# Lp pooling, p = 2: the last, smallest store is queued on SP behind two held stores instead of on ScalarE

## The chip, the cores and the metric

The kernel runs on one core of one Trainium2 chip. The metric is the device time of one execution in microseconds (us). Within one batch of runs the kernel before varied from 395.26 to 395.89 us, so differences below about 0.5 us (0.13%) can't be read from single times; for those the traces are compared piece by piece.

## The reference

For an array `x` of 32 x 256 x 4096 float32, each window of four neighbours gives the square root of the mean of its squares. 134.22 MB are read and 33.55 MB written.

```python
for i in range(out_length):                      # out_length = 1024, kernel_size = 4, p = 2
    window = np.abs(x[:, :, 4*i : 4*i+4]) ** p
    result[:, :, i] = (np.mean(window, axis=-1)) ** (1.0 / p)
```

## The kernel before

The input is seen as 32 blocks of 128 partitions x 8192 elements (4 MB each). SP (SyncE) loads the blocks, ScalarE squares half a block at a time, VectorE adds groups of four, and ScalarE takes the square root, one half block behind. Blocks are grouped for the stores: seven groups of four blocks (4 MB of output each), one of three (3 MB), and the last block alone (1 MB, 8 KB per partition). The stores of groups 0 to 5 are issued on ScalarE. The stores of groups 6 and 7 are *held*: SP issues them after all its loads. The last store (group 8) is on ScalarE.

```python
    groups += [(j, 1) for j in range(n - LAST, n)]
    held = {len(groups) - 1 - LAST - j for j in range(2)}       # groups 6 and 7
    # ... (pools and helpers cut) ...
    def root(i, c):
        # ... o is this half block's part of the group's output tile ot ...
        nc.scalar.activation(
            out=o, in_=o, func=mybir.ActivationFunctionType.Sqrt, scale=1.0 / k,
        )
        if i == first + g - 1 and c + CH == W and group_of[i] not in held:
            nc.scalar.dma_start(out=out_block(group_of[i]), in_=ot)
    # ... main loop: load(i + 3), square, reduce, root of the half block before ...
    root(*pending)
    for gi in sorted(held):
        nc.sync.dma_start(out=out_block(gi), in_=ots[gi])
```

Of the kernel before, what the change touches and what calls it, by code (L numbers as in the profile page):

```python
# [1 line left out]

# [4 lines left out]


@with_exitstack
def kernel(  # L10
    ctx: ExitStack,
    tc: tile.TileContext,
    x: bass.AP,
    p: float,
    kernel_size: int,
    out: bass.AP,
):








    nc = tc.nc

    assert float(p) == 2.0, "kernel specialized for p == 2"
    k = int(kernel_size)
    assert k == 4, "kernel specialized for kernel_size == 4"  # L30

    P = nc.NUM_PARTITIONS
    fp32 = mybir.dt.float32
    xf = x.rearrange("b c l -> (b c l)")
    of = out.rearrange("b c l -> (b c l)")
    total = xf.shape[0] // P

    W = 8192
    CH = 4096
    GROUP = 4  # L40
    LAST = 1
    n = total // W
    assert n * W == total


    groups = []
    i = 0
    while i < n - LAST:
        g = min(GROUP, n - LAST - i)
        groups.append((i, g))  # L50
        i += g
    groups += [(j, 1) for j in range(n - LAST, n)]
    held = {len(groups) - 1 - LAST - j for j in range(2)}
    group_of = {}
    for gi, (first, g) in enumerate(groups):
        for j in range(g):
            group_of[first + j] = gi

    in_pool = ctx.enter_context(tc.tile_pool(name="in_pool", bufs=4))
    out_pool = ctx.enter_context(tc.tile_pool(name="out_pool", bufs=2))  # L60
    last_pool = ctx.enter_context(tc.tile_pool(name="last_pool", bufs=1))
    ctx.enter_context(tc.manual_schedule())


    def x_block(i):
        first, g = groups[group_of[i]]
        block = xf[first * W * P:(first + g) * W * P].rearrange("(p w) -> p w", p=P)
        return block[:, (i - first) * W:(i - first + 1) * W]

    def out_block(gi):  # L70
        first, g = groups[gi]
        return of[first * W * P // k:(first + g) * W * P // k].rearrange("(p w) -> p w", p=P)

    xts = {}
    ots = {}

    def load(i):
        xt = in_pool.tile([P, W], fp32)
        nc.sync.dma_start(out=xt, in_=x_block(i))  # L79
        xts[i] = xt  # L80

    def root(i, c):
        first, g = groups[group_of[i]]
        ot = ots[group_of[i]]
        at = ((i - first) * W + c) // k
        o = ot[:, at:at + CH // k]
        nc.scalar.activation(  # L87
            out=o, in_=o, func=mybir.ActivationFunctionType.Sqrt, scale=1.0 / k,
        )
        if i == first + g - 1 and c + CH == W and group_of[i] not in held:  # L90
            nc.scalar.dma_start(out=out_block(group_of[i]), in_=ot)

    for i in range(3):
        load(i)

    pending = None
    for i in range(n):
        if i + 3 < n:
            load(i + 3)
        gi = group_of[i]  # L100
        first, g = groups[gi]
        if i == first:
            pool = last_pool if i >= n - LAST else out_pool
            ot = pool.tile([P, g * W // k], fp32)
            ots[gi] = ot
        for c in range(0, W, CH):
            xh = xts[i][:, c:c + CH]
            nc.scalar.activation(  # L108
                out=xh, in_=xh, func=mybir.ActivationFunctionType.Square,
            )  # L110
            at = ((i - first) * W + c) // k
            nc.vector.tensor_reduce(  # L112
                out=ots[gi][:, at:at + CH // k],
                in_=xh.rearrange("p (n j) -> p n j", j=k),
                axis=mybir.AxisListType.X, op=mybir.AluOpType.add,
            )
            if pending is not None:
                root(*pending)
            pending = (i, c)
    root(*pending)  # L120
    for gi in sorted(held):
        nc.sync.dma_start(out=out_block(gi), in_=ots[gi])


# [1 line left out]
_INS = ['x', 'p', 'kernel_size']  # L126
_OUTS = [((32, 256, 1024), 'float32')]

_NUMBERS = {'p': 2.0, 'kernel_size': 4}


# [26 lines left out]
```

## Time and profile before

| | before |
|---|---|
| median time | 395.74 us (395.67 to 395.85, 3 runs) |
| span of the profiled execution | 393.7 us |
| share of 16 DMA engines' span taken by both data queues | 83.9% + 15.5% = 99.4% |
| ScalarE (ACT), VectorE (DVE) busy | 75%, 72% |
| last square root ends | 387.23 us |
| last store: issued, landing | 387.26 us, 5.6 us after its issue |

From the page of the kernel before: engine totals, the DMA row (tenths of the mean busy share, 40 slices of the span), and the DMA queues (q1 belongs to SP, q10 to ScalarE; packets, MB, share of 16 engines' span).

```profile
span 393.7 us, 357 instructions
DVE 282.8 (72%) x64; ACT 294.7 (75%) x130; POOL 0.2 (0%) x4
...
DMA  8999998999999999999999999999999999999997
...
q1 hardware_dynamic: 4896, 141.56, 83.9%
q10 hardware_dynamic: 1008, 26.21, 15.5%
...
out_dram<-ot SPq DMA_DIRECT2D x1, 3072.0 KB, 12.3
out_dram<-ot ACTq DMA_DIRECT2D x1, 1024.0 KB, 5.6
```

The DMA engines are the limit: they are busy for 90% or more in all but the first, the seventh and the last slice. The last two lines give size and time from issue to landing (the moment at which the completion of the transfer shows in the trace) of the 3 MB store and of the last store. Only the end of the span can react to this change, so here is the timeline of that end (start, duration, engine, line, what; in brackets the idle time before it and who ended it).

```profile
377.27 8.87 DVE L112 TENSOR_REDUCE ot<-xt 128x1024 f32<-128x4096 f32 x2 [0.84 <-ACT xt L108]
378.09 3.60 ACT L108 ACTIVATE xt<-xt 128x4096 f32<-128x4096 f32 x1
381.72 1.06 ACT L87 ACTIVATE ot<-ot 128x1024 f32<-128x1024 f32 x1
386.17 1.06 ACT L87 ACTIVATE ot<-ot 128x1024 f32<-128x1024 f32 x1 [3.40 <-DVE ot L112]
387.26 0.34 ACTq L91 DMA_DIRECT2D out_dram<-ot  x1
```

Last comes what SP waits for (total us, times, longest us): line 122 is the held stores, line 153 the end of the program.

```profile
SPq L122 <- ACT ot L87: 30.2, 2, 28.7
SPq L153 <- DMA out_dram<-ot: 14.1, 2, 9.6
```

The trace also records each DMA packet (start, duration, queue, size), which is where the end can be watched in detail. It doesn't name the DMA engine, so an engine's sequence has to be matched by ends and starts (they lie within 8 ns of each other). "Runs out" below means the end of an engine's last 24 KB packet of the 3 MB store; the time given is that of the engine's completion record there.

### The profile page before, as it was taken

What the parts mean: (1) busy time and instruction counts of PE and PEld (TensorE: products, weight loads), DVE (VectorE), ACT (ScalarE), POOL (GpSimd) and SP (SyncE); (2) the same over time, 40 slices, a digit from 0 to 9 for tenths busy, and PEclk for the clock granted to TensorE, in tenths of its full rate; (3) what the DMA queues carried; (4) which work ended last, traced back from release to release, by engine and by line L of the source; (5) the groups of instructions that cost most, each with busy time, mean ns of one, the idle gap of its engine ahead of it and who ended that gap; (6) DMA issues with size and microseconds to landing.
All of it is one profiled execution on the core that took longest, in us unless ns stands there. A gap on an engine that the chain in (4) does not pass through costs nothing.

```text
span 393.7 us, 357 instructions
## 1 busy us (share of the span) xinstructions
DVE 282.8 (72%) x64; ACT 294.7 (75%) x130; POOL 0.2 (0%) x4
## 2 busy tenths in 40 slices
DVE  0399996739976399764988559866598846999992
ACT  1699987469883798828988189863998819999981
POOL 0000000000000000000000000000000000000000
DMA  8999998999999999999999999999999999999997
GB/s 350 446 430 426 426 426 373 449 446 430 433 426 426 426 430 453 440 430 433 426 426 426 426 449 443 427 433 430 426 426 426 443 446 433 430 433 426 426 435 314
DMA packets 5906, 167.79 MB, mean 426 GB/s; under 512 B 656, under 2 KB 656, under 8 KB 656
## 3 DMA queue, kind: packets, MB, share of 16 engines
q1 hardware_dynamic: 4896, 141.56, 83.9%
q10 hardware_dynamic: 1008, 26.21, 15.5%
q14 instruction: 2, 0.02, 0.0%
HBM read 134.22 MB, written 33.55 MB: 426 GB/s over the span
## 4 chain that ended last, share of the span: by engine, by line
DMA 72%; ACT 17%; DVE 9%; SPq 0%; issue 0%; ACTq 0%
DMA xt<-in_x_dram 72%; ACT xt L108 14%; DVE ot L112 9%; ACT ot L87 2%; SPq L79 0%; ACTq L108 0%
## 5 line engine op out<-in xcount | busy, mean ns | idle before, releaser
L112 DVE TENSOR_REDUCE ot<-xt 128x1024 f32<-128x4096 f32 x64 | 282.8, 4420 | 103.4 <-ACT xt L108 102.6
L108 ACT ACTIVATE xt<-xt 128x4096 f32<-128x4096 f32 x64 | 230.9, 3610 | 87.6 <-DMA xt<-in_x_dram 85.0
L87 ACT ACTIVATE ot<-ot 128x1024 f32<-128x1024 f32 x64 | 67.0, 1047 | 4.2 <-DVE ot L112 3.4
L108 ACT ACT_TABLE_LOAD x1 | 1.3, 1283 | 0.7 <-PEq L139 0.7
L87 ACT ACT_TABLE_LOAD x1 | 1.3, 1283 | 0.0
L139 POOL MEMSET const-uint8-127<- 128x1 uint8 x1 | 0.1, 102 | 0.0
L139 POOL MEMSET const-bfloat16-1.0<- 128x1 bf16 x1 | 0.1, 101 | 0.0
L139 POOL MEMSET const-float32-0.0<- 128x1 f32 x1 | 0.1, 98 | 0.2 <-issue 0.2
L139 POOL MEMSET const-float32-1.0<- 128x1 f32 x1 | 0.1, 98 | 0.0
## 6 DMA issues: line engine op xcount, KB each, us to landing
xt<-in_x_dram SPq DMA_DIRECT2D x32, 4096.0 KB, 35.9
out_dram<-ot ACTq DMA_DIRECT2D x6, 4096.0 KB, 23.2
out_dram<-ot SPq DMA_DIRECT2D x1, 4096.0 KB, 34.1
out_dram<-ot SPq DMA_DIRECT2D x1, 3072.0 KB, 12.3
out_dram<-ot ACTq DMA_DIRECT2D x1, 1024.0 KB, 5.6
```

What stands on the lines that cost most here:

```text
L87: nc.scalar.activation(out=o, in_=o, func=mybir.ActivationFunctionType.Sqrt, scale=1.0 / k,)
L108: nc.scalar.activation(out=xh, in_=xh, func=mybir.ActivationFunctionType.Square,)
L112: nc.vector.tensor_reduce(out=ots[gi][:, at:at + CH // k], in_=xh.rearrange("p (n j) -> p n j", j=k), axis=mybir.AxisListType.X, op=mybir. ...
L139: nc = _bacc.Bacc("TRN2", target_bir_lowering=False, num_devices=1)
```

## The change

The intent is to take the last DMA issue off ScalarE and to let all three late stores follow one another in SP's queue.

```diff
     held = {len(groups) - 1 - LAST - j for j in range(2)}
+    late = held | set(range(len(groups) - LAST, len(groups)))
@@ root()
-        if i == first + g - 1 and c + CH == W and group_of[i] not in held:
+        if i == first + g - 1 and c + CH == W and group_of[i] not in late:
             nc.scalar.dma_start(out=out_block(group_of[i]), in_=ot)
@@ the end
     root(*pending)
-    for gi in sorted(held):
+    for gi in sorted(late):
         nc.sync.dma_start(out=out_block(gi), in_=ots[gi])
```

## The prediction

> **What bounds the kernel now.** The 16 DMA engines. The page's slices show DMA at 0.9 or more almost throughout; its queue table adds up to 99.4% of 16 engines' span (83.9% + 15.5%), 426 GB/s over 393.7 us for 167.79 MB. ACT (75%) and DVE (72%) have slack; the chain of waits is 72% input loads. Only the end could change. The timeline there: last reduction 381.72 to 386.14, last square root 386.17 to 387.23, last store issued on ScalarE 387.26 to 387.60, landing 5.6 us after its issue, closing waits, end 393.7.
>
> **What is removed, added, moved.** One DMA issue leaves ScalarE (0.34 us, the last thing it does), one joins SP (0.34 us, as SP's other two stores take). The instruction order of both builds shows nothing else moved: each transfer keeps its semaphore, and the moved store still waits only for the last root. SP is free by then (its 3 MB store was issued at 378.2 to 378.6) and need not wait for the stores ahead to land. So the issue moves from 387.26 to about 387.3: one cross-engine semaphore step.
>
> **The bytes.** They are the same on the same 16 engines. The Trainium skill, "DMA: Bandwidth & Descriptors", section "Issuing engines are not separate DMA queues", says that transfers run on the same 16 engines whoever issues them, and that only sequencer issue time is saved. The packet records agree: the 3 MB store (24 KB packets, 912 ns) keeps all engines full until 388.94; then 15 run out one by one (the last at about 389.5) and one lags to 390.10. (Records do not name the engine; I match ends with starts.) Each goes straight on to 8 KB packets, with no gap to remove. The lagging engine ends last: its eight packets of 309 ns (2.47 us) begin at 390.11 and end at 392.56, so the handover between queues costs nothing on the engine that decides. The other 15 lose 0.1 to 0.4 us in slowed packets (up to 746 ns) between 389.55 and 390.2, and are still done by 392.0. If one queue removes that, it is off the critical path.
>
> Queueing behind the held stores costs nothing either: the 4 MB one is gone by 382.8, and the 3 MB one is drained first today too.
>
> **On the critical path:** about 0; the semaphore step (estimate +0.05 us) is hidden as long as descriptors arrive before the lagging engine runs out at 390.1 (now the first packet starts at 388.9, 1.3 us after the issue ended).
>
> **Predicted time:** 395.7 us; 8 in 10 between 395.2 and 396.3. Faster by over 2%: 0.5%; within 2%: 99%; slower by over 2%: 0.5%.
>
> **Signs.** Right: the ScalarE issue row of 1,024 KB goes, an SP row of 1,024 KB comes, issued near 387.3, landing in 5.2 to 5.9 us; all 8 KB packets on the first queue, after the 24 KB ones; the last ends near 392.5; the timeline to 387.2 is unchanged. Wrong: SP issues only after another store has landed (after 390); a gap ahead of the 8 KB packets on the lagging engine, or the slowed packets reaching it (up to +0.4 us); a landing under 5 us, meaning that one queue drains faster than two.
>
> **What would make it wrong.** The lag of that engine (0.6 us) may depend on what the queues did; if it vanishes, some 0.5 us is gained and the slowed packets become critical. A hidden limit on transfers queued by SP could delay the last issue. Both are far below 2%.

Its packet times are all 0.08 us late, because a wrong zero point was taken for them (388.94, 390.10, 390.11 and 392.56 should read 388.86, 390.02, 390.03 and 392.48); durations and order are not touched. The timeline's own times are right.

## The result, and the profile after

| | before | after |
|---|---|---|
| median time | 395.71 us (395.51 to 395.85, 6 runs) | 395.59 us (395.32 to 395.83, 6 runs) |
| ratio, 95% interval | | 0.9997 (0.9985 to 1.001): same |
| span of the profiled execution | 393.68 us | 393.30 us |
| last square root starts | 386.17 us | 385.79 us |
| from there to the end of the span | 7.50 us | 7.51 us |

From the page of the changed kernel (the same lines):

```profile
span 393.3 us, 357 instructions
DVE 282.8 (72%) x64; ACT 294.7 (75%) x130; POOL 0.2 (0%) x4
...
DMA  9999999999999999999999999999999999999997
...
q1 hardware_dynamic: 5040, 142.61, 84.5%
q10 hardware_dynamic: 864, 25.17, 14.8%
...
out_dram<-ot SPq DMA_DIRECT2D x1, 3072.0 KB, 12.3
out_dram<-ot SPq DMA_DIRECT2D x1, 1024.0 KB, 5.6
```

1.05 MB moved from q10 to q1, and the landing of the last store is 5.6 us after its issue, as before. The end of the timeline, after:

```profile
376.88 8.87 DVE L113 TENSOR_REDUCE ot<-xt 128x1024 f32<-128x4096 f32 x2 [0.84 <-ACT xt L109]
377.70 3.60 ACT L109 ACTIVATE xt<-xt 128x4096 f32<-128x4096 f32 x1
381.33 1.06 ACT L88 ACTIVATE ot<-ot 128x1024 f32<-128x1024 f32 x1
385.79 1.06 ACT L88 ACTIVATE ot<-ot 128x1024 f32<-128x1024 f32 x1 [3.39 <-DVE ot L113]
386.87 0.33 SPq L123 DMA_DIRECT2D out_dram<-ot  x1
```

Every line is 0.38 to 0.39 us earlier than before, the last issue included. So the whole 0.38 us by which the profiled spans differ lies before the last root, in a part that the change does not touch; behind it the two agree within 0.01 us. SP's waits, after:

```profile
SPq L123 <- ACT ot L88: 38.9, 3, 28.7
SPq L154 <- DMA out_dram<-ot: 5.1, 1, 5.1
```

SP waits for the root in line 123 for 8.7 us more (38.9 against 30.2), and at the end of the program for 9.0 us less (5.1 against 14.1). It is the same idle time, taken in another line: before, SP stood in its closing wait while ScalarE issued the last store.

The packet records of the last microseconds (times in us from the span's start):

| | before | after |
|---|---|---|
| last store's data could start (issue + 0.85 us, measured in the first experiment) | 388.11 | 387.72 |
| first DMA engine runs out of 24 KB packets | 388.85 | 388.43 |
| 15th, and 16th (the lagging one) | 389.43, 390.02 | 389.21, 389.63 |
| 8 KB packets slowed beyond 400 ns (normal: 309 ns) | 14 of 128, up to 746 ns | none |
| last 8 KB packet ends: 15th and 16th engine | 391.93, 392.48 | 391.67, 392.09 |
| from the 16th running out to the end of its last packet | 2.46 | 2.46 |

Eight packets of 309 ns are 2.47 us, which is what the lagging engine needs in both kernels. The slowed packets are gone, but they were on 14 of the 15 engines that had time to spare.

### The profile page after: what moved, and what is told of

Its sections match the earlier page's. It is cut to its first block, busy times and chain, and to the rows that moved or that the text cites. A ratio compares the mean times of both kernels' runs of the same rounds, so it can differ in the third digit from the quotient of the medians. Undisturbed runs are those within 1.5% of the kernel's fastest.

```text
span 393.3 us, 357 instructions
## 1 busy us (share of the span) xinstructions
DVE 282.8 (72%) x64; ACT 294.7 (75%) x130; POOL 0.2 (0%) x4
## 3 DMA queue, kind: packets, MB, share of 16 engines
q1 hardware_dynamic: 5040, 142.61, 84.5%
q10 hardware_dynamic: 864, 25.17, 14.8%
## 4 chain that ended last, share of the span: by engine, by line
DMA 72%; ACT 17%; DVE 9%; SPq 0%; issue 0%; ACTq 0%
DMA xt<-in_x_dram 72%; ACT xt L109 15%; DVE ot L113 9%; ACT ot L88 2%; SPq L80 0%; ACTq L109 0%
```

## The experiments

The theory, called the *backlog theory*: when the last store is issued, the 16 DMA engines still have the 3 MB store to move; they take the last store's packets when they are through with it, from whichever queue; the engine that is furthest behind ends last, and neither issuer nor queue nor a small delay changes that. The rivals: (a) the last store's issue is on the critical path; (b) the null result is two effects that cancel, such as a slower start on SP against a faster drain from one queue; (c) the place in the queue never matters.

### The last store alone, on either engine

The held stores are left out, so groups 6 and 7 are never written. The DMA engines are idle when the last store is issued.

```diff
 # alone on ScalarE: the kernel before, with
-    for gi in sorted(held):
-        nc.sync.dma_start(out=out_block(gi), in_=ots[gi])
 # alone on SP: the changed kernel, with
-    for gi in sorted(late):
+    for gi in sorted(late - held):
```

> The kernel before without its two held stores (4 MB and 3 MB are never written, so the result is wrong on purpose); the last store stays on ScalarE and meets idle DMA engines, since the loads end near 373. Backlog theory (in the full kernel the last store's data wait behind the 3 MB store's): landing falls from 5.6 us to about 4.2 us after the issue (1.2 us to the first packet, 2.5 us for eight packets, 0.4 us to the semaphore), time about 394.2 us. Rival (the last store's own issue and latency set its 5.6 us, backlog or not): landing stays 5.6 us, time about 395.6 us.

> The changed kernel without its two held stores (wrong on purpose): the last store alone, on SP, with idle DMA engines. Theory (SP and ScalarE are equal as issuers, only a semaphore step apart): same time as the run with the last store alone on ScalarE within 0.3 us, issue at most 0.1 us later after the last root. Rival (two effects of about 0.4 us cancel in the full change: SP is slower to start a store, one queue is faster to drain): here only the first is left, so about 0.4 us slower than alone on ScalarE.

Measured: 393.47 us on ScalarE (393.40 to 393.50, 4 runs) and 393.75 us on SP (393.73 to 393.86, 4 runs), against 395.58 us of the kernel before. The end of the timeline and the last store's issue row, alone on ScalarE:

```profile
385.80 1.06 ACT L87 ACTIVATE ot<-ot 128x1024 f32<-128x1024 f32 x1 [3.40 <-DVE ot L112]
386.89 0.34 ACTq L91 DMA_DIRECT2D out_dram<-ot  x1
```

```profile
out_dram<-ot ACTq DMA_DIRECT2D x1, 1024.0 KB, 3.9
```

And alone on SP:

```profile
386.00 1.06 ACT L88 ACTIVATE ot<-ot 128x1024 f32<-128x1024 f32 x1 [3.40 <-DVE ot L113]
387.08 0.34 SPq L123 DMA_DIRECT2D out_dram<-ot  x1
```

```profile
out_dram<-ot SPq DMA_DIRECT2D x1, 1024.0 KB, 3.9
```

Without a backlog the landing falls from 5.6 to 3.9 us: 1.7 of the 5.6 us were spent waiting behind the 3 MB store. The first packet starts 0.85 us after the start of the issue on both engines (387.74 and 387.93), and from the last root's start to the end of the span it takes 5.82 us on both. So a store on SP is as fast as one on ScalarE, and rival (b) has nothing left to cancel in that part. The 0.28 us between the medians is within the stated 0.3 us, but it is consistent from run to run; 0.20 us of it lies before the last root in the profiled runs (386.00 against 385.80), and the rest lies outside the span. Why that part differs was not looked into.

The time fell by 2.1 us in all: 1.7 us of it from the last root on (5.82 against 7.50 us), and the other 0.4 us before the last root, which starts at 385.80 here and at 386.17 in the profiled run of the kernel before.

The expected size was off: 1.4 us less landing time was expected, and 1.7 was measured, since I took 1.2 us to the first packet. That number came from the full kernel, where the engines were busy at that time, so it was only an upper bound.

### The last store ahead of the held ones

```diff
-    for gi in sorted(late):
+    for gi in [8, 6, 7]:
```

> The changed kernel with SP's late stores in the order last, 4 MB, 3 MB: the last store is ahead of the held ones. Theory: SP's queue is in order and the first wait holds everything behind it, so 8.4 MB of stores are issued after the last root at 387; DMA idles from about 374 to 388.5 and then needs 19.5 us (8.4 MB at 430 GB/s): last packet near 408, time about 411 us (409.5 to 412.5). Rival (place in the queue does not matter, as in the change itself): 395.6 us.

Measured: 410.98 us (410.85 to 411.12, 2 runs), ratio 1.0389 (1.0369 to 1.041), correct. The windows of this run (busy us of each engine with the number of instructions, granted clock, DMA share, GB/s):

```profile
core 0: us, DVE busy (x) ACT busy (x) POOL busy (x), PEclk, DMA share, GB/s
370.00:374.00 4.00, 3.97 (x2) 3.43 (x3) 0.00 (x0) 1.00 0.33 139
374.00:388.00 14.00, 11.01 (x3) 9.52 (x5) 0.00 (x0) 1.00 0.02 9
```

and its issues:

```profile
386.98 1.77 SPq L123 DMA_DIRECT2D out_dram<-ot  x3
```

All three stores are issued in one run after the last root, and the DMA engines stand still for the 14 us before it (share 0.02). Rival (c) falls: the place in SP's queue does matter. It costs nothing in the change only because the last store is behind two stores that can be issued earlier than it anyway.

### A later issue of the last store

In the changed kernel ScalarE makes one, two or four extra in-place copies of the last tile after the last root, and the store waits for them.

```diff
     root(*pending)
+    for _ in range(1):       # 1, 2 or 4
+        o = ots[len(groups) - 1][:, W // k - CH // k:]
+        nc.scalar.activation(out=o, in_=o, func=mybir.ActivationFunctionType.Copy)
```

> The changed kernel with one extra in-place copy of 128x1024 on ScalarE after the last root (about 1.06 us), so that the last store is issued 1.06 us later. Backlog theory, with the 0.85 us from issue to first packet that the two runs with the store alone showed: the data could start at 388.8, the first DMA engine runs out at 388.4 and the lagging one at 389.6, so the engine that ends last loses nothing: 395.6 us, at most +0.2. Rival (the issue is on the critical path): +1.06 us, 396.65 us.

> Two extra copies, 2.1 us later. Backlog theory: the data could start at 389.85, just after the lagging engine runs out at 389.64, last packet near 392.4 in place of 392.1: about +0.3 us, 395.9 us (395.7 to 396.3). Rival: +2.1 us, 397.7 us.

> Four extra copies, 4.25 us later. Backlog theory: all DMA engines are idle before the data start at about 392.0, last packet 2.65 us later at 394.6 in place of 392.1: +2.5 us, 398.1 us (397.7 to 398.5), landing 3.9 us after the issue as alone. Rival: +4.25 us, 399.85 us.

The ends of the three timelines. One copy:

```profile
386.04 1.06 ACT L88 ACTIVATE ot<-ot 128x1024 f32<-128x1024 f32 x1 [3.40 <-DVE ot L113]
387.12 1.06 ACT L124 ACTIVATE ot<-ot 128x1024 f32<-128x1024 f32 x1
388.20 0.33 SPq L126 DMA_DIRECT2D out_dram<-ot  x1
```

Two copies:

```profile
387.01 2.14 ACT L124 ACTIVATE ot<-ot 128x1024 f32<-128x1024 f32 x2
389.18 0.33 SPq L126 DMA_DIRECT2D out_dram<-ot  x1
```

Four copies:

```profile
387.19 4.32 ACT L124 ACTIVATE ot<-ot 128x1024 f32<-128x1024 f32 x4
391.54 0.33 SPq L126 DMA_DIRECT2D out_dram<-ot  x1
```

| | later by | first 8 KB packet | 16th engine runs out | landing after issue | last root's start to end of span | median time |
|---|---|---|---|---|---|---|
| the change | 0 | 388.44 | 389.63 | 5.6 us | 7.51 us | 395.59 us |
| one copy | 1.06 us | 389.03 | 389.89 | 4.5 us | 7.56 us | 395.48 us (4 runs) |
| two copies | 2.14 us | 390.01 | 389.77 | 3.8 us | 7.96 us | 395.87 us (4 runs) |
| four copies | 4.32 us | 392.37 | 389.94 | 3.9 us | 10.14 us | 398.23 us (4 runs) |

The kernel before took 395.62 us in these rounds; the change itself was not run again in them. The ratio to it was 0.9997 (0.9983 to 1.001) with one copy, 1.0008 (0.9994 to 1.0021) with two and 1.0068 (1.0053 to 1.0084) with four. Rival (a) foretold 396.65, 397.7 and 399.85 us. Delaying the issue by 1.06 us costs nothing that shows: the landing time shrinks by as much as the issue is late. With two copies the data arrive 0.24 us after the lagging engine has run out, and the end begins to move (0.45 us more after the root; the time alone is not clear of noise). With four, the whole delay counts except for the slack: 4.32 us later, 2.63 us longer (10.14 less 7.51). So the slack of the last issue was about 1.7 us by this difference, and 1.9 us by the packet records (389.63 less 387.72). The 0.2 us between the two figures is the drain itself: with four copies, on idle engines, the store takes 2.68 us from its first packet's start to its last one's end (392.37 to 395.04), against 2.46 us on the lagging engine. No delay was added in the kernel before, with its issue on ScalarE; its packet records give the same slack of 1.9 us (390.02 less 388.11). The change's own shift of the issue is far inside it.

### Two queues the other way round, and one queue on ScalarE

These two ask where the slowed packets came from, and check that their coming and going costs no time. In both, ScalarE issues the 3 MB store; the last store is on SP (swapped) or on ScalarE as well (both).

```diff
 # swapped: the changed kernel, with
-        if ... and group_of[i] not in late:
+        if ... and group_of[i] not in (6, 8):
-    for gi in sorted(late):
+    for gi in (6, 8):
 # both on ScalarE: the kernel before, with
-        if ... and group_of[i] not in held:
+        if ... and group_of[i] != 6:
-    for gi in sorted(held):
+    for gi in (6,):
```

> The 3 MB store on ScalarE, the last store on SP behind the 4 MB store only: two queues at the end again, the other way round. ScalarE's issue of the 3 MB store stands ahead of the last square, so the last root comes about 0.3 us later. Theory: 395.6 us within 0.4 us, the lagging DMA engine still ends last near 392.3. If the slowed 8 KB packets (over 400 ns) come from a switch of queue, they are back (15 to 20 of 128), off the critical path; if they come from ScalarE's queue alone, they are absent.

> Both the 3 MB store and the last store on ScalarE, the 4 MB store on SP: the last store follows the 3 MB store in one queue, but on the other engine than in the change. ScalarE's issue of the 3 MB store pushes the last root 0.3 us later, as in the swapped run. If slowed 8 KB packets come from the handover between two queues, there are none here (0 of 128 over 400 ns), and first starts follow the 24 KB ends; if they come with ScalarE's queue, some 10 to 15 are there. Time in both: 395.6 us within 0.4 us.

Measured: swapped 395.56 us (395.46 to 395.68, 4 runs), ratio 1.0 (0.9985 to 1.0015) in rounds where the kernel before took 395.58; both on ScalarE 395.39 us (395.31 to 395.69, 4 runs), ratio 0.9995 (0.998 to 1.001) with 395.71 for the kernel before. The ends of the timelines, swapped:

```profile
386.40 1.06 ACT L88 ACTIVATE ot<-ot 128x1024 f32<-128x1024 f32 x1 [3.54 <-DVE ot L113]
387.48 0.34 SPq L123 DMA_DIRECT2D out_dram<-ot  x1
```

Both on ScalarE:

```profile
386.52 1.06 ACT L87 ACTIVATE ot<-ot 128x1024 f32<-128x1024 f32 x1 [3.54 <-DVE ot L112]
387.61 0.34 ACTq L91 DMA_DIRECT2D out_dram<-ot  x1
```

| last two stores on | 8 KB packets over 400 ns | longest | median time |
|---|---|---|---|
| SP, then ScalarE (before) | 14 of 128 | 746 ns | 395.71 us |
| SP, SP (after) | 0 | 318 ns | 395.59 us |
| ScalarE, then SP (swapped) | 10 of 128 | 1447 ns | 395.56 us |
| ScalarE, ScalarE (both) | 0 | 311 ns | 395.39 us |

Slowed packets are there in both runs whose last two stores lie in different queues, and in neither run where one queue has both. Passing to another queue is not enough by itself, though: 2 of the 16 engines before and 6 in the swapped run had none, and the slowed packet was an engine's third 8 KB packet before and its first in the swapped run. In both runs every slowed packet ended only after the lagging engine had run out: at 390.08 to 390.41 us before (it ran out at 390.02), at 389.87 to 390.14 us swapped (389.73). Whether the lag has a part in the slowdown was not tested, and what inside the DMA engine slows the packets is not shown by these records.

Some expectations missed. Fewer packets were slowed in the swapped run (10, not 15 to 20), but by more, and one of the slowed engines ended last, at 392.28 us, 0.10 us after the lagging one (392.18). So the slowdown can reach the end of the kernel, by an amount too small for the time to show. And ScalarE's issue of the 3 MB store delayed the last root by 0.5 us, not by 0.3: from the start of the reduction near 377 us to the last root it takes 9.43 us in both runs, against 8.91 us in the change. From the last root to the end of the span it then took only 7.10 us (swapped) and 6.98 us (both), against 7.51: once more a later last store had its delay taken up by the backlog. In none of the four does the time differ by more than the noise.

### Trying to take the lag away

In the traces with half blocks, one DMA engine falls behind in the load that completes near 259 us (before: 1.8 us between the 15th and the 16th completion, against 0.05 us in the load before it) and keeps 0.4 to 0.8 us of it to the end. An 8 KB packet of the instruction queue runs at 250.8 us, shortly before. Fewer instructions might take it away. In the first run blocks 1 to 29 are squared, reduced and rooted whole; in the second, only blocks 1 to 25.

```diff
+    def ch(i):
+        return W if 1 <= i < n - 2 else CH      # second run: n - 6
-        for c in range(0, W, CH):
+        for c in range(0, W, ch(i)):
 # and ch(i) in place of CH in the slices of square, reduction and root
```

> The changed kernel with one square, one reduction and one root for a whole block of 8192 in blocks 1 to 29 (the last two blocks keep halves): 58 fewer instructions on ScalarE and 29 fewer on VectorE. In every trace so far one DMA engine falls behind just after an 8 KB instruction fetch near 250.5 us and stays behind by 0.4 to 0.8 us to the end. Theory (that fetch makes the lag, and the lagging engine decides the end): if fewer instructions take the fetch away, the lag (16th minus 15th completion) falls below 0.2 us and the time by 0.3 to 0.6 us, to about 395.1 us. If the fetch stays, the lag stays and the time is 395.6 us. If the fetch goes and the lag stays, the lag has another cause.

> As the run with whole blocks, but the last six blocks keep halves, so that ScalarE is not behind at the end and the last root comes near 387 again (it came at 389.15 there, and the store then met idle DMA engines). Backlog theory, with the lag gone as in that run: the last packet ends 2.5 us after the last 24 KB packet, near 391.7, and the time is 395.0 to 395.4 us, about 0.3 us under the kernel before. If the lag is back (0.4 us or more between 15th and 16th completion), 395.6 us and the lag does not depend on the number of instructions as assumed.

Measured: 396.06 us in the first (395.88 to 396.36, 5 runs; ratio 1.0012, 1.0 to 1.0025), where the kernel before took 395.62. The lag was 0.04 us at the end, but ScalarE came late: the last store was issued at 389.17 us, and its first packet started at 390.00, while the last engine had run out at 389.20. That is the delay experiment again, unintended. From the page's issues of this run:

```profile
out_dram<-ot SPq DMA_DIRECT2D x1, 1024.0 KB, 3.9
```

3.9 us is the landing of a store that meets idle engines. In the second run (395.18 us, 394.87 to 395.77, 5 runs; ratio 0.9989, 0.9976 to 1.0001, with 395.71 for the kernel before) the last store came in time (issued at 386.82) and the lag at the end was 0.23 us. Its median is 0.5 us under the kernel before, but the interval includes no change, so it is not shown to be faster; its profiled execution was the slowest of the five. The theory that the fetch makes the lag is not settled either: one of the two fetches remained in both runs, at 261.2 us, and left no lasting lag; nor did the fetch at 159.8 us in the kernel before (0.04 us of lag in the next load); and in the second run a lag of 0.3 us was there well before its fetch.

## Why the prediction was right

- **The bound, and no more than the tail at stake.** Right: 99.4% of the DMA engines' span before, 84.5% + 14.8% = 99.3% after. Only the 7.5 us from the last root on were within reach, 1.9% of the time, so a gain of 2% was out of the question whatever the mechanism; what tests the mechanism is the delays, not the unchanged time.
- **"One cross-engine semaphore step", from 387.26 to about 387.3.** It was not even that: 0.03 us from the last root's end to the issue, on ScalarE (387.23 to 387.26) as on SP (386.84 to 386.87).
- **SP is free and need not wait for the stores ahead.** Right: SP issued the last store at 386.87, while the 3 MB store was still moving until 389.63.
- **The same bytes on the same 16 engines.** Right, and here the Trainium skill, "DMA: Bandwidth & Descriptors", section "Issuing engines are not separate DMA queues", agrees with the runs: 5.82 us from the last root to the end with either issuer when the store is alone, 7.50 and 7.51 us with the backlog. Its addition that several issuers save only sequencer time agrees as well; here even the 0.34 us issue had slack.
- **The engine that decides is the lagging one, and the two-queue slowdown is off its path.** Right for these two kernels: 14 slowed packets became none, and the lagging engine took 2.46 us in both. It does not hold for any two queues: in the swapped run a slowed engine ended last, by 0.10 us.
- **"Hidden as long as descriptors arrive before the lagging engine runs out."** Right, and the delays measured it: nothing to be seen at 1.06 us, a beginning at 2.14 us, 2.63 of 4.32 us.
- **Mis-sized: 1.3 us from the issue's end to the first packet.** Alone it was 0.51 us (0.85 us from its start). The 1.3 us had been read where the engines were busy. The slack was therefore larger than the prediction could see, and the time was not affected.
- **"The timeline to 387.2 is unchanged."** Its durations and order are; it lies 0.39 us earlier in the profiled execution, and so do the last issue (386.87) and the end of the last packet (392.09, against 392.48). The kernel before scatters by as much (spans of 393.3 to 393.8 us in its runs).
- **Possible cause of an error: the lag vanishes.** It did not: 0.59 us before, 0.42 us after. The trace shows it already at the load that lands near 259 us, long before the changed instruction.

## What to carry to other kernels

Before moving a last transfer to another queue, ask what the DMA engines are doing when it is issued. Here they still had a backlog, so neither the issuer nor a delay of 1.06 us counted, and part of the time from issue to landing was waiting (5.6 us, against 3.9 us alone). What did count is which issue stands in front of which wait in an in-order queue: the same three stores with the latest one first cost 15 us more. When two profiled spans differ by a few tenths of a microsecond, measure from the last common instruction before the change, since the part before it scatters by as much.

## What the Trainium skill lacked or had wrong

- "DMA: Bandwidth & Descriptors", section "Latency and other measured facts", gives about 600 ns to the first byte for a transfer issued from SP or ScalarE and does not say from where it is counted. Here it was 0.85 us from the start of the issue, or 0.51 us from its end, on both engines alike, with idle DMA engines.
- The same page, section "Queues, rings and completion order", describes how an engine takes turns between queues, but not that packets can slow down where one queue follows the other: with the last two stores in different queues, 14 of 128 packets took over 400 ns (up to 746) in one run and 10 of 128 (up to 1447) in another; with both in one queue none did, in two runs; 309 ns is normal.
- The same page, section "Bandwidth", has a table of sizes for loads issued from GpSimd only, with 6.15 us for 1 MB. A 1 MB store issued from SP or ScalarE with nothing else moving took 2.66 us from its first to its last packet (387.74 to 390.40), and 3.9 us from issue to landing.
- "Runtime: NRT & Kernel Launch", section "Instruction fetch mechanics", speaks of refills in blocks of 16 KiB. In these traces instruction packets are 8 KB, two of them in mid-kernel (159.8 and 250.8 us before); how many make up a refill they don't show. For transfers issued from SP and ScalarE no page gives a reason why one DMA engine stays behind the others (0.4 to 0.8 us here from 259 us to the end); its cause stayed open.
